# Attention to output projection: a fixed tail order, six prepared operand blocks, the last group's pieces spread by tick

## The chip, the cores and the metric

The kernel runs on one core of one Trainium2 chip. A core has TensorE (PE, the matrix multiplier), VectorE (DVE), ScalarE (ACT), GpSimd (POOL) and SyncE (SP), which here only issues DMAs. The metric is device time in microseconds of one execution. The kernel before has a median of 2857.04 us over 3 runs (2854.59 to 2858.03).

## The reference

Two post-norm layers with different token mixers, on x of 1024 positions by 1024 channels, all in fp32. What the change touches is the first layer's mixer and the projection behind it:

```python
proj = (x @ w_in).reshape(B, S, N_GROUPS, 3, ATTN_HEADS, ATTN_HEAD_DIM)
for g, (window, dilation) in enumerate(((128, 1), (512, 4), (2048, 16))):
    q = rotary(proj[:, :, g, 0], pos)
    k = rotary(proj[:, :, g, 1], pos)
    o, lse = dilated_window_attention(q, k, proj[:, :, g, 2], window, dilation)
wts = softmax(lse over the three g)               # per position and head
o = sum over g of wts[g] * o[g]
y = o.reshape(B, S, 1024) @ w_out
x = layer_norm(ALPHA * x + y)
# then: squared-ReLU MLP, norm; HGRN2 mixer, norm; MLP, norm
```

Each query of dilation d sees itself and 128 keys (or what there are) at distances d, 2d and so on. There are 16 heads of 64 channels.

## The kernel before, in words

Heads are taken in pairs (128 channels, one tile). A **unit** is one pair at one dilation; 24 units are worked in 12 groups of two. The input projection of a group is 21 **products** (252 in all, numbered n); each is 12 matmuls of 128x512 (L666 to L668: high by high, low by high and high by low part of fp32 operands that `split` makes, ACT for the high half at L137, DVE for the low at L138). Seven combined products stand for eight quarter blocks, and DVE and ACT put them together into e (q and k before rotary, L701) and vT.

While a group's products run, the attention of the group before is worked between them. The functions of that work are:

- `rope`: four DMAs on SP copy e with its halves exchanged into rot; DVE multiplies by cos into qT or kT (L472), multiplies rot by sin (L473) and adds (L474). With dilation 4 the DVE writes are strided.
- `pieces`: qk (L500, PE) gives s; a DVE instruction, called stt here, adds the mask and takes the maximum (L511); ACT takes exp (L514); ptr (L524) transposes p on PE; pv (L539) multiplies by v; ACT copies out to og (L547, L550); vtrans transposes v. Six pieces are one unit's `core`.
- `combine_tr`: transposes the statistics (mpt on PE) and sends them through DRAM (mdram) into ml.
- `combine` and `combine_mul` are the mix of a pair's three dilations: maxima, exp, sum, reciprocal and products on rows of 16 (L592 to L605), split into fh and fl (L611), six DMAs on SP spread them out into frow (L616), PE broadcasts a row to the heads' channels (fb, L626), DVE multiplies og by it and adds (L627 to L630).

Each of these steps is put at a product by tables of offsets from the group's base: `ROPES`, `OFFS`, `STATS` and `MIX`, and `ROPES0` for the rope steps of the last group's units, as far as they come before its end. In that loop `in_order` ties PE and DVE to the order in which the code issues; SP, ACT and POOL are ordered by a scheduler.

The **tail** is the attention of the last group's two units (a, dilation 4, and b, dilation 1), the last mixes and the output projection. Mixed output goes to DRAM by pair, in blocks oN[k]; `Out.load` reads a block back (onr) and `split_k` splits it (aoh, aol); the weight blocks wor are loaded and split by `load_w` and `split_w` (woh, wol), in halves of 512 columns (dm 0 and 1). One output tile (t, dm) of 128x512 is the sum over k of three matmuls (`rows`, L183 to L185). `stage_a` makes partial sums with the blocks that are there: tiles (0,0), (1,0), (2,0) side by side over six blocks, then (0,1), (1,1), (2,1), (3,0), (3,1) one by one, and adds ALPHA times the residual into z (L933). After each block's three matmuls `tick` runs some of the waiting steps, from lists that are spread evenly:

```python
ticks = 3 * nka + 5 * 7
def tick():
    count[0] += 1
    while fill and count[1] * ticks < count[0] * total:
        for f in fill.pop(0):
            f()
        count[1] += 1
```

`order.__exit__()` comes before the tail, so there the scheduler chooses the order of all engines. `fin(t)` makes a tile's remaining blocks and its layer norm, `tr(t)` the transposes for the MLP. Three blocks' first half (PREA = 3) are loaded and split in the last products; the others as the tail begins. U takes one of NSLOT = 50 buffers of 4 KB a partition; wp holds p-like work tiles in 3 buffers.

Of the kernel before, what the change touches and what calls it, by code (L numbers as in the profile page):

```python
# [10 lines left out]
F32R = mybir.dt.float32r  # L11
# [5 lines left out]
P = 128  # L17
# [12 lines left out]
RMS_EPS = 1e-6  # L30
CH = 64
NCH = S // CH
NSLOT = 50
NPRE = 2
PREA = 3
SPILL = (6, 5)
NKA = (6, 7)
EARLY = (2, 0)
# [16 lines left out]
       (30, 31, 33, 34, 35, 37, 38, 39, 41, 41, 42, 42, 42, 43))  # L55
STATS = ((12, 13, 15), (21, 22, 24))
ROPES = ((-5, -3, -3, -1, 1, 2), (5, 7, 7, 9, 11, 11))
ROPES0 = ((-5, -2, -1, 2), (-4, 0, 1, 4))
OFFS = ((1, 3, 5, 7, 9, 11), (10, 12, 14, 16, 18, 20))


# [1 line left out]
def trunk_kernel(  # L63
# [24 lines left out]
    nc = tc.nc  # L88
    cp = ctx.enter_context(tc.tile_pool(name="cp", bufs=1))
    up = ctx.enter_context(tc.tile_pool(name="up", bufs=NSLOT))  # L90
    wp = ctx.enter_context(tc.tile_pool(name="wp", bufs=3))
    sp = ctx.enter_context(tc.tile_pool(name="sp", bufs=4))
    ps = ctx.enter_context(tc.tile_pool(name="ps", bufs=1, space=bass.MemoryType.PSUM))
    dp = ctx.enter_context(tc.tile_pool(name="dp", bufs=1, space=bass.MemoryType.DRAM))
# [4 lines left out]
    def bank(tag, name):  # L99
        return ps.tile([P, 512], F32, name=name, tag=tag, bufs={"mm": 3, "s": 2, "pt": 2, "o": 1}[tag])  # L100
# [221 lines left out]
    def attention(pre, hc):  # L322
# [150 lines left out]
            return qT, (lambda: nc.vector.tensor_mul(rot, rot, sinT),  # L473
                        lambda: nc.vector.tensor_add(cls(qT, g), cls(qT, g), nat(rot, g)))  # L474

        def pieces(pr, g, qT, kT, vT, og, sS):
            st = {}

            def has_prev(b):
# [49 lines left out]

            def pv(b):  # L530
                if b % 4 == 0:
                    st["o"] = bank("o", "o")
                o = st["o"]
                pts = st.pop(("pt", b))
                nb = 2 if has_prev(b) else 1
                for i in range(nb):
                    kb = b - nb + 1 + i
                    for h in range(2):
                        nc.tensor.matmul(o[h * HD:(h + 1) * HD, (b % 4) * P:(b % 4 + 1) * P],  # L539
                                         st["vn"][:, kb * P + h * HD:kb * P + (h + 1) * HD],  # L540
                                         pts[:, (h * nb + i) * P:(h * nb + i + 1) * P],
                                         start=i == 0, stop=i == nb - 1, skip_group_check=True)
                if b % 4 == 3:
                    hb = b // 4
                    d = DIL[g]
                    if d == 1:
                        act(og[:, hb * 512:(hb + 1) * 512], o, AF.Copy)  # L547
                    else:
                        r = d // 2
                        act(og.rearrange("p (n r) -> p r n", r=d)[:, hb * r:(hb + 1) * r, :],  # L550
                            o.rearrange("p (r n) -> p r n", r=r), AF.Copy)

            return [
                [lambda: qk(0), vtrans],
                [lambda: qk(2), lambda: ptr(0), lambda: ptr(1)],
# [150 lines left out]
        def unit_work(gi, a, base):  # L706

            pr, g = groups[gi][a]
            if pr not in ml:
                ml[pr] = small([16, 2, NG, P], "ml", 1)  # L710
                ogs[pr] = [None] * NG
            sS = small([P, 2, 2, 8], "stats", 3)

            adds = {}

            def rope_of(t):
                res[a, t], adds[t] = rope(ep.pop((gi, a, 0 if t == 1 else 1)), g, "qT" if t == 0 else "kT")

            def begin():
                ogs[pr][g] = U("og")  # L720
                p = pieces(pr, g, res.pop((a, 0)), res.pop((a, 1)), ep.pop((gi, 2, a)), ogs[pr][g], sS)
# [18 lines left out]
        order.__enter__()  # L740
        load_x("21", 0, (L, R))
        first_w(0, R)
        load_x("21", 1, (L, R))
# [16 lines left out]
                low_w(n)  # L760
        for n in range(len(seq)):
            gi, i, j = seq[n]
            load_w(n + LOADW)
            if j == 0 and n // 3 < 6:
                get_T(n // 3 + 1, 1)
# [7 lines left out]
                constants2()  # L773
            if n == 36:
                hc.append(hgrn_consts())
            if n == len(seq) - 2 * PREA - 3:
                early = pre(oN)
            if n >= len(seq) - 2 * PREA - 1:
                next(early, None)
            if n == 0:  # L780
                get_T(2, 0)
# [7 lines left out]
            if n % 21 == 14:  # L789
# [3 lines left out]
                for a in range(2):  # L793
# [14 lines left out]
                    for k, f in zip(MIX[a], mix):  # L808
                        at(base + k, f)
                if last:  # L810
                    for a in range(2):
                        for k, f in list(zip(ROPES0[a], tail[a][0])):
                            if k < -1:
                                at(base + k, f)
                                tail[a][0].remove(f)
        order.__exit__()
        (ra, ca, sa, _), (rb, cb, sb_, mx) = tail
        done = [f for n in sorted(fill) for f in fill[n]]
        mine = [[ra[0]], [rb[0], rb[1]], [ra[1]], [ca[0], rb[2]], [ca[1]], [cb[0]], [ca[2]], [cb[1]], [ca[3]], [cb[2]],
                [ca[4]] + sa, [cb[3]], [ca[5]], [cb[4]] + sb_, [cb[5]], mx[:1], mx[1:3], mx[3:5], [],  # L820
                mx[5:7], mx[7:10], mx[10:]]
        lists = [done[k:k + 1] + (mine[k] if k < len(mine) else []) for k in range(max(len(done), len(mine)))]
        return oN, lists


    class Out:
# [9 lines left out]
            self.split_w(k, 0)  # L836

        def pre_steps(self, oN):
            for k in range(PREA):
                self.load(k, oN, 0)  # L840
                raw = U("wor")
                self.w[k] = (None, None, raw)
                nc.sync.dma_start(raw[:, :512], self.w_dram[k][:, :512])

            def steps():
                for k in range(PREA):
                    raw = self.w[k][2]
                    hi, lo = U("woh", F32R), U("wol", F32R)
                    self.w[k] = hi, lo, raw
                    split(raw[:, :512], hi[:, :512], lo[:, :512])  # L850
                    yield
                    self.split_k(k, 0)
                    yield

            return steps()

        def split_w(self, k, dm):
            hi, lo, raw = self.w[k]
# [24 lines left out]
                self.split_k(k, 0)  # L883


    def outproj_ln(pr, oN, fill, resid, gB_ap, bB_ap, keep):
        a = {}
        w = pr.w
        xo = pr.xo
# [6 lines left out]
        for k in range((PREA, NPRE)[pr.mixer], nka):  # L896
            pr.load(k, oN, 0)
            pr.load_w(k)
            split_k(k, 0)
        for k in range(nka):  # L900
            pr.split_w(k, 1)
        z = []

        def load_z(t):
# [11 lines left out]
        ticks = 3 * nka + 5 * 7  # L916

        def tick():
            count[0] += 1
            while fill and count[1] * ticks < count[0] * total:  # L920
                for f in fill.pop(0):
                    f()
                count[1] += 1
# [14 lines left out]
        def second(n):  # L938
            for _ in range(n):
                if ahead and len(oN) > ahead[0]:  # L940
                    k = ahead.pop(0)
                    pr.load(k, oN, 1)
                    split_k(k, 1)

        ks = list(range(nka))
        stage_a([(0, 0), (1, 0), (2, 0)], ks)
        for n, (t, dm) in enumerate([(0, 1), (1, 1), (2, 1), (3, 0), (3, 1)]):
            load_z(max(t, 1) + 1)
            if n in (1, 3) and len(w) < NK:
                k = len(w)  # L950
                pr.load_w(k)
                pr.split_w(k, 1)
            k = len(ks)
            if k < 7 and len(oN) > k and k < len(w):
                pr.raw[k] = oN[k]
                split_k(k, 0)
                ks = ks + [k]
            stage_a([(t, dm)], ks)
            if n >= EARLY[pr.mixer]:
                second(2)  # L960
# [4 lines left out]
        while fill:  # L965
            for f in fill.pop(0):
                f()
        for k in range(len(ks), NK):
# [4 lines left out]
        second(NK)  # L973
        xn = Fast(name + "f")

        def tr(t):
# [15 lines left out]
                nc.sync.dma_start(keep[t * P:(t + 1) * P, :], z[t])  # L992

        fin(0)
        fin(4, (0,))
        fin(1)
        fin(4, (1,))
        fin(2)
        fin(5, (0,))
        fin(3)  # L1000
        tr(0)
        fin(5, (1,))
        tr(1)
        tr(2)
        fin(6, (0,))
# [476 lines left out]
    def hgrn(xs, late, consts, pre, gw):  # L1482
# [101 lines left out]
        for hd in range(8):  # L1584
# [61 lines left out]
            for i in range(3):  # L1646
# [13 lines left out]
    x5d = dp.tile([S, D], F32, name="x5d")  # L1660
    pr = Out(w_attn_out, "a", 0)
    hc = []
    oN, fill = attention(pr.pre_steps, hc)
    xf, late = outproj_ln(pr, oN, fill, lambda t: x[t * P:(t + 1) * P, :],
                          ln_mix_g[0], ln_mix_b[0], x1d)
# [5 lines left out]
    xf, late = outproj_ln(pr, oN, fill, lambda t: x3d[t * P:(t + 1) * P, :],  # L1671
                          ln_mix_g[1], ln_mix_b[1], x5d)
    ffn(1, xf, late, x5d, ln_ffn_g[1], ln_ffn_b[1], True)

# [76 lines left out]
```

## Time and profile before

| what | value |
|---|---|
| median of 3 runs | 2857.04 us (2854.59 to 2858.03) |
| the profiled execution | 2856.82 us; its span 2854.6 us |
| mean granted TensorE clock | 0.995 |
| PE busy | 2789.4 us, 98% of the span |
| DVE, ACT, POOL busy | 2053.8, 1448.4, 122.6 us |
| share of PE in the chain that ended last | 90% |
| last product's last matmul (L668) | starts at 973.19 us |
| first matmul of the output projection (L183) | 973.42 us |

Times in rows of the trace are microseconds from the start of the span. A row of a timeline has the start, the duration, the engine, the line, the operation, and out<-in with the tile's names; in square brackets stand the idle time of the engine before it and what ended that. A row of the list of waits has the total, the number and the longest. A matmul's record lasts 0.39 us though one starts every 0.23 us, since they are pipelined; so what TensorE loses is read from the starts. `L` numbers are those of the kernel before; in the changed kernel the same lines lie 5 to 40 further down.

### The profile page before, as it was taken

Reading aid. Unit: us, or ns where it says so; the run is one execution under the profiler, and the core shown is the slowest. Engines: PE = TensorE matmul, PEld = TensorE weight load, DVE = VectorE, ACT = ScalarE, POOL = GpSimd, SP = SyncE. Lnnn points to the kernel's source line nnn. Section 1 sums busy time; section 2 is a strip of 40 time slices with the busy share of each in tenths; the row PEclk is TensorE's granted clock in tenths of the full one; section 3 lists DMA queues with packets and bytes.
Section 4 is the critical chain, followed back from the end, with each engine's and each line's share of the span. In section 5 each row is a group of like instructions: output and inputs, shape, how many; then the busy total and the mean of one; then the engine's idle time right before and its main releaser. Section 6 shows DMA issues by size and latency. Waiting matters only on the chain.

```text
span 2854.6 us, 39893 instructions
## 1 busy us (share of the span) xinstructions
PE 2789.4 (98%) x14152; PEld 2235.3 (78%) x14152; DVE 2053.8 (72%) x3830; ACT 1448.4 (51%) x3105; POOL 122.6 (4%) x67
## 2 busy tenths in 40 slices
PE   8999999999999989999999999999999999999998
PEld 6777777777777767888878887778787788878887
DVE  7768777776887767786686875555667787678677
ACT  5555555655555555544454444554553645454433
POOL 0000000000000003000000011111102200000000
PEclk9999999999999999999999999999999999999999
DMA  7766665666667523464584843101131455475654
GB/s 291 249 201 193 190 197 171 215 206 204 198 198 222 154 77 133 156 220 156 173 303 126 275 142 104 38 30 60 51 120 71 159 202 174 155 268 189 223 176 132
DMA packets 204935, 485.25 MB, mean 170 GB/s; under 512 B 29376, under 2 KB 43712, under 8 KB 204736
## 3 DMA queue, kind: packets, MB, share of 16 engines
q1 hardware_dynamic: 204736, 482.72, 51.3%
q8 instruction: 111, 1.82, 0.3%
q14 instruction: 88, 0.72, 0.1%
HBM read 362.82 MB, written 94.24 MB: 160 GB/s over the span
## 4 chain that ended last, share of the span: by engine, by line
PE 90%; DVE 4%; ACT 2%; DMA 1%; issue 1%; POOL 0%; SPq 0%; DVEq 0%; POOLq 0%; ACTq 0%
PE pmm L666 8%; PE pmm L668 8%; PE pmm L667 8%; PE pup L1114 7%; PE pup L1112 7%; PE pup L1113 7%; PE pdy L1264 4%; PE pdy L1260 4%; PE pdy L1263 4%; PE pmm L171 3%; PE s L500 3%; PE pdx L1263 3%; PE pdx L1264 3%; PE pdx L1260 3%; PE pmm L173 3%; PE pmm L172 3%
## 5 line engine op out<-in xcount | busy, mean ns | idle before, releaser
L666 PE MATMUL pmm<-xh,H 128*128 128x512 f32 x1008 | 407.7, 404 | 12.0 <-ACT H L432 8.5
L668 PE MATMUL pmm<-xh,H 128*128 128x512 f32 x1008 | 396.4, 393 | 0.0
L667 PE MATMUL pmm<-xl,H 128*128 128x512 f32 x1008 | 396.1, 393 | 0.0
L666 PEld LDWEIGHTS pmm<-xh,H 128*128 128x128 f32 x1008 | 191.2, 190 | 52.3 <-ACT H L432 8.5
L668 PEld LDWEIGHTS pmm<-xh,H 128*128 128x128 f32 x1008 | 190.4, 189 | 41.9 <-DVE H L440 0.3
L667 PEld LDWEIGHTS pmm<-xl,H 128*128 128x128 f32 x1008 | 191.1, 190 | 36.9
L514 ACT ACTIVATE p<-p,stats 128x128 f32<-128x128 f32 (+1 forms) x384 | 168.3, 441 | 92.6 <-DVE stats L511 92.2
L1263 PE MATMUL pdy<-dT,dS 128*128 128x512 f32 x512 | 199.2, 389 | 0.0
L1260 PE MATMUL pdy<-dT,dS 128*128 128x512 f32 x512 | 199.2, 389 | 0.0
L1264 PE MATMUL pdy<-dT,dS 128*128 128x512 f32 x512 | 199.2, 389 | 0.0
L511 DVE CUSTOM_DVE_ANT_0 p<-s,mask 128x128 f32<-128x128 f32 (+1 forms) x384 | 113.2, 347 | 68.4 <-PE s L500 58.8
L137 ACT ACTIVATE dS<-dr 128x512 fp32r<-128x512 f32 x192 | 119.5, 622 | 73.3 <-PE pdy L1264 36.6
L171 PE MATMUL pmm<-f0nh,wh 128*128 128x512 f32 x384 | 153.1, 399 | 0.0
L173 PE MATMUL pmm<-f0nh,wl 128*128 128x512 f32 x384 | 149.8, 390 | 0.0
L172 PE MATMUL pmm<-f0nl,wh 128*128 128x512 f32 x384 | 149.6, 390 | 0.0
L138 DVE TENSOR_TENSOR dS<-dr,dS 128x512 fp32r<-128x512 f32 x192 | 135.1, 703 | 16.5 <-ACT dS L137 16.5
L214 POOL TENSOR_TENSOR z<-z,bB 128x1024 f32<-128x1024 f32 x24 | 58.5, 2442 | 1687.8 <-ACT z L213 1678.3
L527 ACT ACTIVATE pts<-ppt 128x256 f32<-128x256 f32 (+1 forms) x192 | 85.3, 474 | 62.7 <-PE ppt L524 60.5
L137 ACT ACTIVATE dT<-hold 128x512 fp32r<-128x512 f32 x128 | 80.0, 625 | 69.5 <-DVE hold L1239 28.8
L1073 ACT ACTIVATE H<-wc 128x512 fp32r<-128x512 f32 x128 | 77.2, 625 | 74.6 <-DVE wc L1066 43.9
L1263 PEld LDWEIGHTS pdy<-dT,dS 128*128 128x128 f32 x512 | 96.1, 188 | 20.0
L1264 PEld LDWEIGHTS pdy<-dT,dS 128*128 128x128 f32 x512 | 96.1, 188 | 20.0
(395 smaller groups left out, 6927.9 us busy)
## 6 DMA issues: line engine op xcount, KB each, us to landing
xh<-xtd SPq DMA_DIRECT2D x110, 512.0 KB
xl<-xtd SPq DMA_DIRECT2D x110, 512.0 KB
dr<-hd SPq DMA_DIRECT2D x192, 256.0 KB
dr<-in_w_down_dram SPq DMA_DIRECT2D x128, 256.0 KB
rot<-e SPq DMA_DIRECT2D x192, 128.0 KB
wa<-in_w_up_dram SPq DMA_DIRECT2D x48, 512.0 KB
wb<-in_w_attn_dram SPq DMA_DIRECT2D x36, 512.0 KB
wa<-in_w_attn_dram SPq DMA_DIRECT2D x33, 512.0 KB
```

The lines of the kernel that those rows point to most:

```text
L171: nc.tensor.matmul(o, wh[:, k], xs.h(k), start=k == 0, stop=False)
L172: nc.tensor.matmul(o, wh[:, k], xs.l(k), start=False, stop=False)
L173: nc.tensor.matmul(o, wl[:, k], xs.h(k), start=False, stop=k == NK - 1)
L666: nc.tensor.matmul(o, wh, hi[k // 2][:, c], start=begin and k == 0, stop=False, skip_group_check=True)
L667: nc.tensor.matmul(o, wh, lo[k // 2][:, c], start=False, stop=False, skip_group_check=True)
L668: nc.tensor.matmul(o, wl, hi[k // 2][:, c], start=False, stop=end and k == 3, skip_group_check=True)
L1112: nc.tensor.matmul(o, wh, xf.h(b, k), start=begin and k == 0, stop=False, skip_group_check=True)
L1113: nc.tensor.matmul(o, wh, xf.l(b, k), start=False, stop=False, skip_group_check=True)
L1114: nc.tensor.matmul(o, wl, xf.h(b, k), start=False, stop=end and k == 3, skip_group_check=True)
L1260: nc.tensor.matmul(o[q], h, T_[:, L], start=begin, stop=False, skip_group_check=True)
L1263: nc.tensor.matmul(o[q], h, T_[:, R], start=False, stop=False, skip_group_check=True)
L1264: nc.tensor.matmul(o[q], l, T_[:, L], start=False, stop=end, skip_group_check=True)
```

## The change

1. **Order.** PE and DVE stay tied to the issue order to the end of stage A, and SP too from product 228 (PINSP).
2. **Six blocks.** `pre_steps` loads and splits the first half of six onr blocks and all of six wor blocks (one DMA of 128x1024 where there were two of 128x512), one split per product from n = 234 on. One slot less (NSLOT 49), one wp buffer more.
3. **Stage A by single tiles.** (0,0), (1,0), (2,0), (0,1), (1,1), (2,1) with six blocks, then (3,0), (3,1), (4,0), (4,1) with seven: 64 ticks. Each tick has its events: rope, core, statistics, mix, loads, splits.
4. **The last units.** Three of their rope steps come sooner (ROPES0); what is left, the end of kT, is at ticks 1 (a) and 5 (b). Cores are at ticks 3 to 33 and 6 to 36, the last mix at 38 to 55; the pieces take ptr ahead of qk, and the second unit's pv uses a bank of "mm". The mix of the last group but one moves (MIX0), some of it into the first ticks.
5. **The end.** fin and tr in another order; tile 4 is then partly done.

The numbers of PE, DVE and ACT instructions are the same in both kernels.

```diff
-NSLOT = 50
+NSLOT = 49
-PREA = 3
+PREA = 6
+PINSP = 228
-ROPES0 = ((-5, -2, -1, 2), (-4, 0, 1, 4))
+MIX0 = (20, 21, 21, 22, 23, 25, 26, 27, 27, 28, 29, 30, 30, 31)
+ROPES0 = ((-5, -2, -2, 0), (-4, -1, -1, 0))
+TCORE = ((3, 9, 15, 21, 27, 33), (6, 12, 18, 24, 30, 36))
+TROPE = (1, 5)
+TSTATS = ((25, 26, 30), (28, 29, 33))
+TMIX = (38, 40, 41, 43, 44, 48, 49, 50, 51, 52, 53, 54, 55, 55)
...
-    wp = ctx.enter_context(tc.tile_pool(name="wp", bufs=3))
+    wp = ctx.enter_context(tc.tile_pool(name="wp", bufs=4))
...
-                    st["o"] = bank("o", "o")
+                    st["o"] = bank("mm" if last == 2 else "o", "o")
...
+            if last:
+                return [
+                    [lambda: qk(0), vtrans],
+                    [lambda: ptr(0), lambda: ptr(1), lambda: qk(2)],
+                    [lambda: pv(0), lambda: pv(1), lambda: ptr(2), lambda: ptr(3), lambda: qk(4)],
...
+            if n == PINSP:
+                queue.__enter__()
...
-            if n == len(seq) - 2 * PREA - 3:
+            if n == len(seq) - 3 * PREA - 4:
                 early = pre(oN)
-            if n >= len(seq) - 2 * PREA - 1:
+            if n >= len(seq) - 3 * PREA - 4:
                 next(early, None)
...
-        order.__exit__()
...
+        for n in sorted(fill):
+            on([3 * (n - len(seq))] * len(fill[n]), fill[n])
+        on(TROPE, (ra[0], rb[0]))
+        for a, (core, stats) in enumerate(((ca, sa), (cb, sb_))):
+            on(TCORE[a], core)
+            on(TSTATS[a], stats)
+        on(TMIX, mx)
+        return oN, events, (order, queue)
...
         def tick():
+            if orders:
+                for f in fill.pop(count[0], []):
+                    f()
+                count[0] += 1
+                return
...
+            for n, k in enumerate((6, 7)):
+                on(4 + 6 * n, lambda k=k: pr.load_raw(k))
+                for dm in range(2):
+                    on(26 + 12 * n + 2 * dm, lambda k=k, dm=dm: pr.split_raw(k, dm))
+            for k in range(6):
+                on(4 * k, lambda k=k: pr.load(k, oN, 1))
+                on(19 + 3 * k, lambda k=k: split_k(k, 1))
+            for n, k in enumerate((6, 7)):
+                on(32 + 24 * n, lambda k=k: (pr.load(k, oN, 0), split_k(k, 0)))
+                on(34 + 23 * n, lambda k=k: split_k(k, 1))
+            for t, dm in [(0, 0), (1, 0), (2, 0), (0, 1), (1, 1), (2, 1), (3, 0), (3, 1), (4, 0), (4, 1)]:
+                load_z(max(t, 1) + 1)
+                stage_a([(t, dm)], list(range(6 if t < 3 else 7)))
...
         fin(0)
+            fin(1)
+            fin(5, (0,))
+            fin(2)
+            fin(5, (1,))
+            fin(3)
+            tr(0)
+            fin(4)
```

More of the change, by code (lines that the diff above doesn't have):

```diff
@@ L474, in rope, with pieces @@
                         lambda: nc.vector.tensor_add(cls(qT, g), cls(qT, g), nat(rot, g)))
-        def pieces(pr, g, qT, kT, vT, og, sS):
+        def pieces(pr, g, qT, kT, vT, og, sS, last):
             st = {}
@@ L720, in begin @@
                 ogs[pr][g] = U("og")
-                p = pieces(pr, g, res.pop((a, 0)), res.pop((a, 1)), ep.pop((gi, 2, a)), ogs[pr][g], sS)
+                p = pieces(pr, g, res.pop((a, 0)), res.pop((a, 1)), ep.pop((gi, 2, a)), ogs[pr][g], sS,
+                           a + 1 if gi == len(groups) - 1 else 0)
                 for f in p[0]:
@@ L740, in attention @@
         order.__enter__()
+        queue = in_order((mybir.EngineType.SP,))
         load_x("21", 0, (L, R))
@@ L807, in attention @@
                         at(base + k, f)
-                    for k, f in zip(MIX[a], mix):
+                    for k, f in zip(MIX0 if gi == len(groups) - 2 else MIX[a], mix):
                         at(base + k, f)
@@ L812, in attention, with on @@
                         for k, f in list(zip(ROPES0[a], tail[a][0])):
-                            if k < -1:
+                            if k < 0:
                                 at(base + k, f)
                                 tail[a][0].remove(f)
-        order.__exit__()
         (ra, ca, sa, _), (rb, cb, sb_, mx) = tail
[L818 to L823, printed above, removed]
+        events = {}
+        def on(ts, fs):
+            for t, f in zip(ts, fs):
+                events.setdefault(t, []).append(f)
+        for n in sorted(fill):
[6 more added lines that the diff above has]
+        return oN, events, (order, queue)
     class Out:
@@ L838, in pre_steps, with load_raw, split_raw @@
         def pre_steps(self, oN):
[L839 to L855, printed above, removed]
+            for n in range(3 * PREA + 4):
+                k, step = divmod(n, 3)
+                if step == 0 and k < PREA:
+                    self.load(k, oN, 0)
+                    self.load_raw(k)
+                if n >= 4:
+                    k, step = divmod(n - 4, 3)
+                    if step == 1:
+                        self.split_k(k, 0)
+                    else:
+                        self.split_raw(k, step // 2)
+                yield
+        def load_raw(self, k):
+            self.w[k] = (U("wor"),)
+            nc.sync.dma_start(self.w[k][0], self.w_dram[k])
+        def split_raw(self, k, dm):
+            if dm == 0:
+                self.w[k] = (U("woh", F32R), U("wol", F32R)) + self.w[k]
+            hi, lo, raw = self.w[k]
+            c = slice(dm * 512, dm * 512 + 512)
+            split(raw[:, c], hi[:, c], lo[:, c])
+            if dm == 1:
+                self.w[k] = (hi, lo)
         def split_w(self, k, dm):
@@ L883, in pre, with outproj_ln @@
                 self.split_k(k, 0)
-    def outproj_ln(pr, oN, fill, resid, gB_ap, bB_ap, keep):
+    def outproj_ln(pr, oN, fill, orders, resid, gB_ap, bB_ap, keep):
         a = {}
@@ L895, in outproj_ln @@
         nka = NKA[pr.mixer]
[L896 to L901, printed above, removed]
+        if not orders:
+            for k in range(NPRE, nka):
+                pr.load(k, oN, 0)
+                pr.load_w(k)
+                split_k(k, 0)
+            for k in range(nka):
+                pr.split_w(k, 1)
         z = []
@@ L943, in second, with tail, on @@
                     split_k(k, 1)
+        def tail():
+            def on(t, f):
+                fill.setdefault(t, []).append(f)
+            for n, k in enumerate((6, 7)):
[11 more added lines that the diff above has]
+                stage_a([(t, dm)], list(range(6 if t < 3 else 7)))
+            assert not fill, sorted(fill)
+            for o in orders:
+                o.__exit__()
+        if orders:
+            tail()
         ks = list(range(nka))
-        stage_a([(0, 0), (1, 0), (2, 0)], ks)
-        for n, (t, dm) in enumerate([(0, 1), (1, 1), (2, 1), (3, 0), (3, 1)]):
+        if not orders:
+            stage_a([(0, 0), (1, 0), (2, 0)], ks)
+        for n, (t, dm) in enumerate([] if orders else [(0, 1), (1, 1), (2, 1), (3, 0), (3, 1)]):
             load_z(max(t, 1) + 1)
@@ L967, in outproj_ln @@
                 f()
-        for k in range(len(ks), NK):
+        for k in range(len(ks), NK if not orders else 0):
             pr.raw[k] = oN[k]
@@ L972, in outproj_ln @@
         bB = bcast_rows(bB_ap, "bB")
-        second(NK)
+        if not orders:
+            second(NK)
         xn = Fast(name + "f")
@@ L994, in outproj_ln @@
         fin(0)
[L995 to L1002, printed above, removed]
+        if orders:
+            fin(1)
[5 more added lines that the diff above has]
+            fin(4)
+        else:
+            fin(4, (0,))
+            fin(1)
+            fin(4, (1,))
+            fin(2)
+            fin(5, (0,))
+            fin(3)
+            tr(0)
+            fin(5, (1,))
         tr(1)
@@ L1662, in trunk_kernel @@
     hc = []
-    oN, fill = attention(pr.pre_steps, hc)
-    xf, late = outproj_ln(pr, oN, fill, lambda t: x[t * P:(t + 1) * P, :],
+    oN, fill, orders = attention(pr.pre_steps, hc)
+    xf, late = outproj_ln(pr, oN, fill, orders, lambda t: x[t * P:(t + 1) * P, :],
                           ln_mix_g[0], ln_mix_b[0], x1d)
@@ L1670, in trunk_kernel @@
     oN, fill = hgrn(xs, late, hc, pr.pre, gw)
-    xf, late = outproj_ln(pr, oN, fill, lambda t: x3d[t * P:(t + 1) * P, :],
+    xf, late = outproj_ln(pr, oN, fill, None, lambda t: x3d[t * P:(t + 1) * P, :],
                           ln_mix_g[1], ln_mix_b[1], x5d)
```

4 lines of the change are left out of this document (added).

## The prediction

> **What bounds the kernel now.** The page is read first, for the busy shares of the engines.
>
> ```profile
> span 2854.6 us, 39893 instructions
> PE 2789.4 (98%) x14152; PEld 2235.3 (78%) x14152; DVE 2053.8 (72%) x3830; ACT 1448.4 (51%) x3105; POOL 122.6 (4%) x67
> ```
>
> TensorE is busy for 98% of the span, so a change that leaves its matmuls alone can win only where it waits or runs at a lower granted clock. The table of 10-us stretches is read next, over the tail of attention. Its columns are length, busy time (and count) of each engine, granted TensorE clock, DMA share and GB/s.
>
> ```profile
> core 0: us, PE busy (x) PEld busy (x) DVE busy (x) ACT busy (x) POOL busy (x), PEclk, DMA share, GB/s
> 1040.00:1050.00 10.00, 6.42 (x29) 4.58 (x29) 9.44 (x19) 4.60 (x9) 0.00 (x0) 0.92 0.48 161
> 1050.00:1060.00 10.00, 8.13 (x28) 5.79 (x28) 5.87 (x12) 1.57 (x3) 0.00 (x0) 0.84 0.30 81
> 1060.00:1070.00 10.00, 9.38 (x22) 5.74 (x22) 9.07 (x17) 1.28 (x3) 0.00 (x0) 0.56 0.23 84
> ```
>
> The third row is the surprising one: PE is 94% busy, with half the matmuls of a full stretch, because the clock stands at 0.56. Then the waits of TensorE between 972 and 1072 us (total, times, longest), and its timeline for the places.
>
> ```profile
> PE pmm L183 <- ACT aoh L137: 4.0, 2, 3.6
> PE fb L626 <- DMA frow<-fh: 1.9, 1, 1.9
> PE pmm L183 <- DVE z L933: 1.3, 1, 1.3
> PE pmm L183 <- DVE vT L701: 0.8, 1, 0.8
> PE o L539 <- ACT og L550: 0.7, 2, 0.4
> PE s L500 <- DVE kT L474: 0.5, 1, 0.5
> ```
>
> ```profile
> 973.19 0.39 PE L668 MATMUL pmm<-xh,H 128*128 128x512 f32 x1
> 973.42 0.39 PE L183 MATMUL pmm<-woh,aoh 128*128 128x512 f32 x1
> ...
> 1047.61 0.50 PE L183 MATMUL pmm<-woh,aoh 128*128 128x512 f32 x1 [3.58 <-ACT aoh L137]
> ...
> 1048.34 0.80 PE L185 MATMUL pmm<-woh,aol 128*128 128x512 f32 x1
> ...
> 1051.49 0.51 PE L183 MATMUL pmm<-woh,aoh 128*128 128x512 f32 x1
> ...
> 1057.75 0.70 PE L626 MATMUL fb<-frow,bsel 128*128 128x512 f32 x2 [1.87 <-DMA frow<-fh]
> ...
> 1058.52 0.59 PE L184 MATMUL pmm<-wol,aoh 128*128 128x512 f32 x1
> ...
> 1068.51 0.53 PE L185 MATMUL pmm<-woh,aol 128*128 128x512 f32 x1
> ```
>
> The last product of attention starts its last matmul at 973.19; the output projection's first follows at 973.42 (one every 0.23 us at full clock). I call 973.4 T0.
>
> **What the change removes.** The six lines add up to 9.2 us; a wait also leaves some 0.1 us before the next matmul's start, and there are eight, so I take 10. Two stretches run at half clock. From 1048.34 to 1051.49 eight matmuls take 3.15 us instead of 1.8: 1.4 us. From 1058.52 to 1068.51, 19 matmuls (4 of them fb) and one wait of 0.5 us take 10 us instead of 4.3 (19 x 0.227); less that wait, which is in the 10 already, 5.2 us. The new order removes the causes of all six: the operand blocks that aoh L137 split late are split in the last group, z is loaded sooner, and each core piece has a tick of its own. **Removed: 10 + 1.4 + 5.2 = 16.6 us.** That is the most that the tail can give; numbers of instructions on PE, DVE and ACT stay as they are.
>
> **What it adds, wait A.** From here the rows are of VectorE, whose order in the tail is now fixed to the order in which the code issues. They start just ahead of T0.
>
> ```profile
> 970.89 0.28 DVE L511 CUSTOM_DVE_ANT_0 p<-s,mask 128x128 f32<-128x128 f32 x1
> 971.11 2.35 DVE L473 TENSOR_TENSOR rot<-rot,sinT 128x1024 f32<-128x1024 f32 x2
> 973.38 2.05 DVE L474 TENSOR_TENSOR qT<-qT,rot 128x1024 f32<-128x1024 f32 x1
> 975.33 1.03 DVE L701 TENSOR_TENSOR vT<-pmm,vp 128x512 f32<-128x512 f32 x1
> 976.20 0.35 DVE L592 TENSOR_TENSOR mn<-ml 16x128 f32<-16x128 f32 x1
> ...
> 977.08 0.40 DVE L593 TENSOR_TENSOR mn<-mn,ml 16x128 f32<-16x128 f32 x1
> 978.01 0.88 DVE L595 TENSOR_TENSOR ml<-mn,ml 16x128 f32<-16x128 f32 x3
> 978.80 0.67 DVE L138 TENSOR_TENSOR wol<-wor,woh 128x512 fp32r<-128x512 f32 x1
> 979.40 1.21 DVE L474 TENSOR_TENSOR qT<-qT,rot 128x1024 f32<-128x1024 f32 x1
> 980.54 0.54 DVE L598 TENSOR_TENSOR ml<-ml 16x384 f32<-16x384 f32 x1
> 982.81 0.37 DVE L600 TENSOR_TENSOR mn<-ml 16x128 f32<-16x128 f32 x1
> 983.22 0.39 DVE L601 TENSOR_TENSOR mn<-mn,ml 16x128 f32<-16x128 f32 x1
> 983.65 0.94 DVE L603 RECIPROCAL mn<-mn 16x128 f32<-16x128 f32 x1
> 984.62 0.88 DVE L605 TENSOR_TENSOR ml<-ml,mn 16x128 f32<-16x128 f32 x3
> 991.25 2.02 DVE L472 TENSOR_TENSOR kT<-e,cosT 128x1024 f32<-128x1024 f32 x1
> ```
>
> In the kernel before, 18 ticks of matmuls lie between T0 and qk(0) of unit a, so its kT wait is the 0.5 us of the list. In the changed one qk(0) stands at tick 3. Up to it TensorE has 12 projection matmuls (2.7 us), four pv, four ppt and a statistics transpose with the friction between them (1.5 us): it asks for kT at T0 + 4.2 = 977.6.
>
> VectorE's queue in the changed order, from the stt that ends at 971.1 (that one waits for TensorE's s, so it isn't sooner or later than here): one rot product 1.2, the strided qT add 1.95 (973.38 to 975.33), the kT product that was at 991.25 before, 1.9, one wol split 0.6. So vT starts at 976.8, against 975.33. Then vT 0.9; the mix of the last but one group, L592, L593, L595 (x3) 1.6; rot, qT add and kT product of unit b, 1.2 + 1.15 + 1.15; L598, L600, L601, L603, L605 (x3) 0.5 + 0.4 + 0.4 + 0.95 + 0.8; and only then rot 1.2 and the strided kT add 1.95 of unit a. That is 12.2 us, to 989.0. TensorE stands from 977.6 to 989.0, **A = 11.4 us.** Behind it wait vtrans, all later ticks and, through them, ACT and the statistics: nothing else can fill it, for the order of PE is fixed too. Low end 8 us, if VectorE were at vT at T0; high end 13, with a microsecond or two of backlog from the twelve more splits (0.6 each) that now lie in the last group. That backlog I take as nothing: VectorE waited 9.6 us for s between 895 and 955, in the row below, and of its total work little is added ahead of T0, as the later ones drop out of it.
>
> ```profile
> L511 DVE CUSTOM_DVE_ANT_0 p<-s,mask 128x256 f32<-128x256 f32 (+1 forms) x20 | 6.5, 379 | 9.6 <-PE s L500 9.6
> ```
>
> **Half clock behind A.** Both long waits above (3.6 and 1.9 us) were followed within about a microsecond by a stretch at half clock. One of 3.2 to 3.4 us costs 1.4 to 1.7. I take **1.6**; the ends are 0.9 and, by the long stretch, 5.1.
>
> The Trainium skill (TensorE: Matmul & The Clock Gate, Part 1: The HAM clock gate) has one idle window of about 3.4 us close the gate and one busy window open it, in a free-running window. The trace agrees on the length of a stretch (1048.34 to 1051.49) but shows 1.87 us to be enough for a drop at 1058.5. By the page's rule as it stands A drops the clock once and B, below, perhaps not at all; the sum would be 1.6 us lower.
>
> **Small ones.** qk(0) of unit b at tick 6 comes out even: kT of b is ready about 4 us after A ends, TensorE is there in 4.2. A ppt behind the first fb must wait for the og product, since there are two such banks: 0.9 us (fb, then one product of 0.7 and its start). The second unit's pv has a bank of its own now, so the L550 wait doesn't come back. One slot less and a fourth wp buffer: nothing, as each wor block is split soon after it lands.
>
> **Wait B, at tick 48.** The last mix starts on VectorE behind the z addition of tick 35; call its end on PE X. z 0.6, L592 to L595 1.6, two splits 1.2, L598 to L605 3.05, one z 0.6, fl 0.55: 7.6 us. Then the issues on SP and the landing.
>
> ```profile
> 1055.63 0.61 SPq L616 DMA_DIRECT2D frow<-fl  x1
> ```
>
> Six issues stand 0.65 us apart, of which the first is out ahead of fl: X + 10.6 for the start of the last. From 1055.63 to the fb at 1057.75 it took 2.1 us: X + 12.7. TensorE has 12 ticks of 0.68 us and 1.6 us of pv until it needs fb: X + 9.8. **B = 2.9 us**, between 2 and 4 (a split or a z addition more or less on the chain, and the issue's spread), and half clock behind it, at the short stretch's price, **1.6** (0 to 5.1; the fb's lie a tick apart now, so the short one is nearer).
>
> **Sum.** Added: 11.4 + 1.6 + 0.9 + 2.9 + 1.6 = 18.4 us. Removed: 16.6. The end of the tail (fin, the transposes) has the same work in another order and I cost that at nothing: VectorE is the same number of instructions behind the last z. Net +1.8 on the profiled execution's 2856.8 us (span 2854.6 and 2.2 around it), which is 0.2 below the median of 2857.0: **2858.6 us.** With the bounds (added 8 + 0.9 + 0.9 + 2 to 13 + 5.1 + 0.9 + 4 + 5.1) the sum goes from -4.8 to +11.5.
>
> **The rivals.** The measurement can tell 0.2%, that is 5.7 us, from no change.
>
> *Forecast, no change within 0.2%:* A takes what the six waits gave. For it: A's terms are rows, and the order is fixed. 0.42.
>
> *Slower: the clock stays low.* Where it decides: the first 10 us behind A. There TensorE has qk, eight transposes and short ppt's with DVE and ACT between them, and at 1058.5 such a mixture, after only 1.87 us of idling, kept half clock for 10 us instead of 3.2. If any wait of 0.5 us lies there (kT of b is even to within that), the long price comes twice: 2 x 3.5 us more, 2858.6 + 7 = 2866. Against it: more 128x512 matmuls lie between than at 1058. 0.35, with late loads on the SP queue, whose order is now fixed from the 229th product on, in the same case.
>
> *Faster: A at its floor and no B.* A is 8 us if VectorE comes to vT at T0; B goes if fl comes 3 us sooner, as it would if the z additions and the two splits in its way (2.4 us) were done while VectorE waits, and its half clock goes with it. 8 + 1.6 + 0.9 - 16.6 = -6.1: 2850.7. Against it: VectorE had no idle time from 970.9 to 985, so A's queue can't well be shorter. 0.23.
>
> *It doesn't do what it says:* the six blocks are split but wor lands late, and aoh or woh L137 is waited for again. 512 KB per block is asked for 7 products ahead; it is within the slower case.
>
> **How the numbers follow.** The range takes the forecast's bounds and the larger part of both rivals: 2847 to 2868. Chances: faster 0.23, same 0.42, slower 0.35.
>
> **What would show it.** Right: one wait of s on DVE kT of about 11 us that starts near 977, with the granted clock at half behind it; no wait on aoh L143 near 1043; one of fb on frow of 2 to 4 us near tick 48; 44 matmuls in 10 us elsewhere. Wrong: a kT wait under 8 us (the VectorE queue was misread, then the change is faster by the difference), or stretches at 0.5 clock that last over 5 us (slower), or waits of the products ahead of T0, which the kernel before doesn't have.

## The result and the profile after

The changed kernel takes **2863.24 us** (median of 12 runs, 2858.84 to 2867.85), the kernel before 2857.31 in the runs beside it: ratio 1.0021, 95% interval 1.0012 to 1.0030. That is 5.9 us or 0.21% slower, just past the 0.2% that I took as the bound of no change. The forecast was 2858.6, so 4.6 us are to be explained. The profiled execution is the slowest of the twelve: 2867.85 us, 11.0 more than before's.

The first page lines of the changed kernel:

```profile
span 2866.1 us, 39906 instructions
PE 2787.6 (97%) x14152; PEld 2237.8 (78%) x14152; DVE 2052.1 (72%) x3832; ACT 1448.7 (51%) x3105; POOL 121.7 (4%) x67
```

TensorE has as many instructions as before and is busy for 1.8 us less, so all of the difference is waiting or clock. (VectorE has two instructions more, 3832 for 3830: additions into z, of which the new stage A makes 18 where there were 16.) Its 10-us stretches (columns as in the prediction):

```profile
940.00:950.00 10.00, 7.30 (x41) 5.83 (x39) 6.12 (x15) 6.26 (x16) 0.00 (x0) 0.79 0.68 249
950.00:960.00 10.00, 10.00 (x61) 7.76 (x60) 6.59 (x16) 6.81 (x20) 0.00 (x0) 0.87 0.48 148
...
980.00:990.00 10.00, 5.51 (x31) 3.74 (x29) 9.86 (x13) 1.95 (x8) 0.00 (x0) 1.00 0.93 296
990.00:1000.00 10.00, 2.89 (x14) 2.24 (x15) 8.54 (x20) 1.33 (x6) 0.00 (x0) 0.51 0.11 42
...
1060.00:1070.00 10.00, 7.60 (x28) 6.20 (x29) 5.60 (x9) 0.63 (x1) 0.00 (x0) 0.83 0.45 162
...
1110.00:1120.00 10.00, 8.10 (x41) 6.39 (x40) 4.63 (x11) 5.42 (x13) 2.40 (x1) 0.99 0.62 217
```

Two of these four holes were forecast: 980 to 1000 with half clock in it (wait A) and 1060 to 1070 (wait B). Two were not: 940 to 960, ahead of the tail, and 1110 to 1120, in the end of it. TensorE's waits between 972 and 1080 us confirm the first two:

```profile
PE s L506 <- DVE kT L480: 11.4, 1, 11.4
PE fb L641 <- DMA frow<-fh: 2.8, 1, 2.8
PE ppt L530 <- ACT pts L533: 0.9, 1, 0.9
PE ppt L530 <- DVE og L642: 0.7, 1, 0.7
```

Where the time went is read from the starts of the same matmul in both traces. First the kernel before: product 228, the 193rd matmul of the projection, the first of the MLP. Up to the 193rd, TensorE has the same matmuls of each kind in both kernels.

```profile
879.95 0.48 PE L666 MATMUL pmm<-xh,H 128*128 128x512 f32 x1
...
1070.03 0.39 PE L183 MATMUL pmm<-woh,aoh 128*128 128x512 f32 x1
...
1118.34 0.39 PE L1112 MATMUL pup<-af11h,H 128*128 128x512 f32 x1
```

Then the same three and others of the changed one:

```profile
880.43 0.48 PE L681 MATMUL pmm<-xh,H 128*128 128x512 f32 x1
...
946.36 1.97 PE L545 MATMUL o<-pts,vn 128*64 128x128 f32 x16 [2.70 <-ACT og L553]
...
980.88 0.39 PE L683 MATMUL pmm<-xh,H 128*128 128x512 f32 x1
...
997.11 1.66 PE L506 MATMUL s<-kT,qT 64*128 64x128 f32 x8 [11.35 <-DVE kT L480]
...
1075.38 0.39 PE L189 MATMUL pmm<-woh,aoh 128*128 128x512 f32 x1
...
1119.32 0.50 PE L189 MATMUL pmm<-woh,aoh 128*128 128x512 f32 x1 [1.90 <-DVE z L1054]
...
1126.49 0.39 PE L1186 MATMUL pup<-af11h,H 128*128 128x512 f32 x1
```

| stretch | before | changed | difference | forecast |
|---|---|---|---|---|
| product 228 to the last product's last matmul | 93.2 | 100.5 | **+7.2** | 0 |
| from there to the 193rd matmul of the projection | 96.8 | 94.5 | **-2.3** | +1.8 |
| from there to the MLP's first matmul | 48.3 | 51.1 | **+2.8** | 0 |

Behind that the MLP's first 336 matmuls lose 1.2 us more and what follows, to the start of the last matmul, 2.5 (1643.6 to 1646.1). Several of these items change from run to run. In other kernels whose products are the same, the first stretch took 98.5 to 99.3 us, and the last part 1642 to 1645. In act_order, sp_free and mix_sooner, below, whose end is the same, the third stretch took 49.2 to 49.4 us, only 0.9 to 1.1 more than before, and the MLP lost nothing: their waits for z of 1.6 to 1.7 us left the clock at 1.00. With 98.5 for the first stretch and nothing for the last part the sum is 5.3 - 2.3 + 2.8 + 1.2 = 7.0 us, and with the cheaper end 5.3 - 2.3 + 1.0 = 4.0; the medians' 5.9 lies between.

### The profile page after: what moved, and what is told of

It reads as the page before. It is cut to its first block, busy times and chain, and to the rows that moved or that the text cites. A ratio compares the mean times of both kernels' runs of the same rounds, so it can differ in the third digit from the quotient of the medians.

```text
span 2866.1 us, 39906 instructions
## 1 busy us (share of the span) xinstructions
PE 2787.6 (97%) x14152; PEld 2237.8 (78%) x14152; DVE 2052.1 (72%) x3832; ACT 1448.7 (51%) x3105; POOL 121.7 (4%) x67
## 3 DMA queue, kind: packets, MB, share of 16 engines
q1 hardware_dynamic: 203584, 482.71, 51.1%
```

## The experiments

Two theories stood at the start. **Mine:** three separate places, products 237 to 243 (ACT and DVE, loaded with the early splits), the late z in fin, and waits A and B as forecast. **The rival:** one cause, SP's fixed order, which makes loads late everywhere. All ratios below are to the kernel before in the same runs.

**The hole at 943 us.** ACT's and DVE's timelines of the changed kernel show what stood ahead of pv:

```profile
943.70 0.60 ACT L712 ACTIVATE e<-pmm 128x512 f32<-128x512 f32 x1 [2.12 <-PE pmm L683]
944.20 1.14 ACT L143 ACTIVATE aoh<-onr 128x512 fp32r<-128x512 f32 x2
945.24 0.59 ACT L710 ACTIVATE e<-pmm 128x512 f32<-128x512 f32 x1
945.71 0.60 ACT L553 ACTIVATE og<-o 128x512 f32<-128x512 f32 x1
```

```profile
944.85 0.69 DVE L144 TENSOR_TENSOR aol<-onr,aoh 128x512 fp32r<-128x512 f32 x1 [3.84 <-ACT aoh L143]
945.46 0.42 DVE L517 CUSTOM_DVE_ANT_0 p<-s,mask 128x256 f32<-128x256 f32 x1
```

pv needs the o bank, which the og copy empties; ACT had put that copy behind an e copy that waits 2.1 us for TensorE's own product, and behind two splits of the early blocks. DVE stood 3.84 us for the same aoh, with the stt behind it.

*act_order.* `in_order` for ACT as well, from product 228 to the last one:

```diff
+        loop = in_order((mybir.EngineType.Activation,))
...
+                loop.__enter__()
...
+        loop.__exit__()
         (ra, ca, sa, _), (rb, cb, sb_, mx) = tail
```

> ACT too is tied to the issue order from product 228 to the last product (not in the tail). Theory: the 2.7 us in which pv waited for og L553 at 943 us, with half clock behind it, came because ACT's order had the copy to og behind an e copy that waits for TensorE's next product, and two aoh splits of the early blocks behind the same copy. Then the last 15 products come back by 4 to 7 us: 2857 to 2860. Rival, the data of the early blocks come late because SP's order is fixed from product 228: aoh still waits, no gain, about 2863. A third possibility, ACT in issue order waits in other places: later than 2865.

Measured: 2862.65 us, ratio 1.0017 (1.0008 to 1.0026). The og wait went, and others came. Waits of TensorE from 900 to 1000 us:

```profile
PE s L506 <- DVE kT L480: 11.2, 1, 11.2
PE o L545 <- ACT pts L533: 3.1, 3, 1.6
PE mpt L579 <- ACT pts L533: 2.2, 2, 1.8
```

The stretch from product 228 still took 98.5 us. The order of ACT chooses which wait is seen; it isn't what makes the loss. The time is the rival's, but not by the rival's way, since the wait that it was to keep has gone.

*sp_free.* SP left to the scheduler (the three lines of `queue` out).

> SP is left to the scheduler; PE and DVE stay tied. Theory: SP's fixed order isn't what costs: same waits, 2861.5 to 2864.5. Rival: loads pass the waiting stores and rot copies, and the waits of products 237 to 243 or the kT wait go: under 2860.

Measured: 2862.59 us, 1.0016 (1.0007 to 1.0025), the same waits to 0.2 us. The rival theory falls: SP's fixed order costs nothing here that these runs can tell.

*late_splits.*

```diff
-            if n == len(seq) - 3 * PREA - 4:
+            if n == len(seq) - 11:
                 early = pre(oN)
-            if n >= len(seq) - 3 * PREA - 4:
+            if n >= len(seq) - 11:
+                next(early, None)
                 next(early, None)
```

> The early blocks' 18 splits are made at two per product from n = 243 to 251 instead of one per product from 234 on; loads start at n = 241. Theory: the 18 extra splits on ACT and DVE, not one queue's order, hold ptr, s, H and og of products 237 to 243 up, 5.3 us with half clock behind the longest (tying ACT's order only moved that to other waits). Without them there, these products come back to the pace of the kernel before: 3 to 5 us, 2858.5 to 2860.5. Rival: VectorE and ACT are as full in 243 to 251, the loss moves there or into the wait for kT at tick 3: 2862 to 2865.

Measured: 2863.28 us, 1.0022 (1.0012 to 1.0032). Product 228 and the last product of late_splits, then its waits:

```profile
881.90 0.48 PE L681 MATMUL pmm<-xh,H 128*128 128x512 f32 x1
...
975.69 0.39 PE L683 MATMUL pmm<-xh,H 128*128 128x512 f32 x1
```

```profile
PE s L506 <- DVE kT L480: 14.6, 1, 14.6
```

93.8 us, all but 0.6 of the loss is gone: the splits in products 237 to 243 are its cause. And the rival that I gave with it is right as well: the kT wait is 3.2 us longer, the stretch from the last product to the 193rd matmul 6.3 longer (100.8), the wait for z in fin 3.3 us instead of 1.9, and the time is the same. VectorE has to make these splits before kT in either case; they are paid where they are put.

**Wait A.** *mix_sooner:* MIX0 begins (17, 18, 18, 19, 20, 25, ...).

> The first five mix steps of the last group but one (L607 to L631) come three products sooner (MIX0 17, 18, 18, 19, 20). Theory: the 11.4 us wait for kT at tick 3 is the sum of VectorE's queue, 5.6 us of which are these steps; VectorE was busy for only 4.3 us between 960 and 970. The wait falls to 6 to 9 us and the time by 2.5 to 5.5 us: 2858 to 2861. Rival, VectorE comes to the last vT later by as much: wait and time unchanged, 2863.

Measured: 2864.96 us, 1.0030 (1.0018 to 1.0042). From 900 to 1000 us:

```profile
PE s L506 <- DVE kT L480: 8.0, 1, 8.0
PE o L545 <- ACT og L553: 2.7, 1, 2.7
PE o L545 <- ACT pts L533: 1.1, 1, 1.1
PE ppt L530 <- ACT p L520: 1.0, 2, 0.9
```

The kT wait fell as the sum says, within the 6 to 9 us given, but pv and ppt ahead of it waited about 2 us that they had not, vtrans behind it 0.7, and the time did not fall.

*cores_later:* TCORE, TSTATS, TMIX and block 7 by 12 ticks, tiles (5, 0) and (5, 1) in stage A, z of tile 7 sooner.

> Both last units' cores, statistics, mix and block 7 come 12 ticks later, and stage A makes tile 5's partial sums as well (78 ticks); residual 7 is asked for after fin(1), as in z_sooner. To compare with z_sooner, 2859.4. Theory: qk(0) reaches TensorE 8.2 us later, VectorE's 12.2 us are done meanwhile: the kT wait falls from 11.3 to about 3 us, half clock behind it goes, and the later mix has room enough: 8 to 10 us less, 2849 to 2852. Rival: the whole chain of the last mix ends later, and fin of block 7 waits for it: 2858 to 2861.

Measured: 2869.47 us, 1.0046 (1.0033 to 1.0058). Its waits from 972 to 1080 us:

```profile
PE fb L641 <- DMA ml<-mdram: 9.6, 1, 9.6
PE fb L641 <- DMA frow<-fl: 5.3, 1, 5.3
```

VectorE's and SP's timelines ahead of the first of them, whose fb starts at 1003.38:

```profile
998.07 0.53 DVE L626 TENSOR_TENSOR fl<-ml,fh 16x384 fp32r<-16x384 f32 x1
```

```profile
1001.30 0.61 SPq L631 DMA_DIRECT2D frow<-fl  x1
```

No wait for kT at all, and 9.6 us at the next thing that VectorE makes: the first fb of the older mix, at tick 12. (The list names a load of ml, which SP issues only at 1002.39. What fb reads is frow, whose last copy goes out at 1001.30, behind an fl that VectorE makes straight after kT.) Both expectations missed, and the miss tells the most. While kT was the wait, that fb lay behind it and was never late.

*later_all* moves the older mix too (first step at tick 6, fb from tick 30), the last mix's fb five ticks more, block 6 to tick 50 and 7 to 76, with tiles 0 to 6 over six blocks each; *later_all_late* is the same with the splits of late_splits and cores 15 ticks later.

> As cores_later, 12 ticks later, but with what held that one up moved too: the whole mix of the last group but one (first step at tick 6 instead of 0, its fb from tick 30 instead of 12), the last mix's fb five ticks more, block 6 split at tick 50, block 7 at 76; stage A makes tiles 0 to 6 with six blocks each (84 ticks), z of 6 and 7 is asked for within it. The early splits stay at one per product. To compare with fb_and_z, 2855.5. Theory: the 11.3 us wait for kT is time in which VectorE's 12.2 us lie on the path; with 5.6 us of mix behind them and 8.2 us of matmuls beside them nothing is left of it, and the half clock behind it goes: 2842 to 2846. Rival: VectorE's total work is the bound of the stage, the wait comes back at qk(0) of b or at an fb: 2852 to 2857.

> The same with the early splits of late_splits (two per product from n = 243) and cores 15 ticks later. Theory: in late_splits the 5.3 us of products 237 to 243 came back and were lost again at the kT wait (14.6 for 11.4) and beside it; now that wait is covered but for about 3 us, so the products' 5 us stay won: 2839 to 2844. Rival: VectorE stays behind through the first 20 ticks, qk of a and b wait 5 us or more: 2846 to 2852.

Measured: 2857.76 us, 1.0000 (0.9991 to 1.0009), and 2860.31, 1.0009 (1.0000 to 1.0018). Of the waits of later_all from 972 to 1080 us the two long ones:

```profile
PE s L506 <- DVE stats L517: 4.2, 1, 4.2
PE vpt L494 <- ACT vn L495: 1.4, 1, 1.4
```

The kT wait's 11.4 us are down to 5.6, but the time is just above the rival's range (2852 to 2857) and far from the theory's 2842 to 2846. Against fb_and_z, below, nothing is left of the gain: the fuller end waits for POOL's norm, z and the MLP's weights instead (POOL z 1.6, z 1.3, DVE H 2.6 and ACT H 1.7 us). later_all_late missed both of its expectations: the products are back at 93.8 us, TensorE waits 3.1 us for s, 1.8 and 1.6 at ppt and z in stage A, and why it comes out 2.5 us behind later_all stays open.

**Wait B and the late z.** *fb_later:* the last mix's fb at ticks 53 to 60, block 7 at 61.

> The last mix's broadcasts (fb) and the split of block 7 come five ticks later (TMIX 53 to 60 for 48 to 55). Theory: fb waits 2.8 us for frow at tick 48 and half clock follows; five ticks are 3.4 us of matmuls, so both go: 2859 to 2860. Rival, the wait moves to the end of stage A or to fin, which needs block 7 (aoh L143): 2863 or later.

Measured: 2857.84 us, 1.0003 (0.9994 to 1.0012): 5.4 us less than the changed kernel, and no fb wait.

*z_sooner:*

```diff
             fin(1)
+            load_z(7)
             fin(5, (0,))
```

> The residuals of tiles 6 and 7 are asked for after fin(1) instead of in fin(6) and fin(7). Theory: they stood on SP behind the sixth store to x1d, which the new order of fin makes later; z L1054 held TensorE for 1.9 us at 1117 and half clock followed. Both go, 2 to 4 us: 2859 to 2861. Rival, the MLP's weights are still behind the stores and are the next wait: 2862 to 2863.

Measured: 2859.39 us, 1.0006 (0.9997 to 1.0015), 3.9 less, with no z wait. SP's timelines show where the loads stood, before and changed:

```profile
1076.88 25.07 SPq L992 DMA_DIRECT2D x1d<-z  x6
1102.04 1.21 SPq L907 DMA_DIRECT2D z<-in_x_dram  x2
```

```profile
1087.57 25.69 SPq L1057 DMA_DIRECT2D x1d<-z  x6
1113.32 1.25 SPq L942 DMA_DIRECT2D z<-in_x_dram  x2
```

In both the last two z loads stand behind six stores; TensorE is 5.4 us later at 1075, the loads are 11.3 us later, since the sixth store (1101.63 before, 1112.94 changed) waits for a norm that the new order of fin makes last. VectorE's row of the changed kernel shows who waited for them:

```profile
1118.58 1.29 DVE L1054 SCALAR_TENSOR_TENSOR z<-z,pmm 128x512 f32<-128x512 f32 x2 [2.82 <-DMA z<-in_x_dram]
```

*fb_and_z*, both edits:

> fb_later and z_sooner together. Theory, two separate places: -5.4 and -3.9 add up, about 2854 (2853 to 2856). Rival, the two share a cause (in fb_later the z wait was 1.5 us instead of 1.9): about 2857.

Measured: 2855.47 us, 0.9990 (0.9981 to 0.9999). The two add up to within 1.5 us (their sum would be 2853.9), so they are two places, as the theory had it.

**A version that is faster than both.** *gap_splits* is fb_and_z with

```diff
-                next(early, None)
+                for _ in range(1 if n < 240 else 0 if n < 244 else 1 + n % 2):
+                    next(early, None)
```

> fb_and_z (2855.5) with the early steps one per product to n = 239, none at 240 to 243, then one and two in turn from 244 to 251. Theory: the waits of products 237 to 243 come from the splits right there; VectorE and ACT have 2 to 4 us free in each of the products 244 to 249, so about 4 of the 5.3 us come back and the kT wait grows by 1 to 2 us: 2852 to 2854. Rival, as late_splits showed, VectorE gives all of it back at kT: 2855 to 2857.

Measured: **2853.53 us, 0.9984 (0.9976 to 0.9993)**, with 11 runs between 2852.93 and 2855.05. Two waits of gap_splits:

```profile
PE s L506 <- DVE kT L480: 11.6, 1, 11.6
PE o L545 <- ACT og L553: 1.7, 1, 1.7
```

The og wait is 1 us shorter and the kT wait has grown by only 0.3 us. The stretch from product 228 is 97.0 us. In fb_and_z it took 99.3, with half clock behind the og wait, and in fb_later, where the clock stayed at 1.00, 98.5: so 1.5 us are gained beside the clock. The medians of gap_splits and fb_and_z lie 1.9 us apart, but their runs overlap (fb_and_z: 2851.60 to 2858.72), so the size of this last step is less sure than that gap_splits beats both kernels.

*gap_and_3:* gap_splits with cores, statistics and the last mix three ticks later.

> gap_splits with cores and statistics three ticks later and the last mix as much (fb 56 to 62, block 7 at 63). Theory: the kT wait falls by the 2 us of matmuls, as far as VectorE is its only bound: 2 us under gap_splits. Rival: the end of the mix, now at the last ticks, holds fin (aoh L143) up by as much: no difference to gap_splits.

Measured: 2853.36 us, 0.9983 (0.9974 to 0.9992). The time is the rival's, no difference, but not by its way, since no wait for aoh in fin appears: kT waits 2.6 us less (9.0), and og (1.9 us more), fb (0.8) and z (0.4) take it back.

## Why the prediction missed its size

- **What bounds the kernel** was right: TensorE's busy time didn't move (2787.6 for 2789.4 us) and the whole difference lies in waits and clock.
- **Wait A** was right in place, cause and size: forecast 11.4 us, measured 11.4. VectorE's queue came out step by step:

```profile
979.15 1.22 DVE L479 TENSOR_TENSOR rot<-rot,sinT 128x1024 f32<-128x1024 f32 x1
...
984.76 1.06 DVE L716 TENSOR_TENSOR vT<-pmm,vp 128x512 f32<-128x512 f32 x1
...
993.92 1.20 DVE L479 TENSOR_TENSOR rot<-rot,sinT 128x1024 f32<-128x1024 f32 x1
995.15 1.91 DVE L480 TENSOR_TENSOR kT<-kT,rot 128x1024 f32<-128x1024 f32 x1
```

  From the rot product to vT 5.6 us (forecast 5.65), from vT to the end of kT 12.3 (12.2). TensorE asked for kT at 985.8, 4.7 us behind its T0 of 981.1 (forecast 4.2).
- **Wait B** was right: forecast 2.9, measured 2.8 us. The half clock behind A and B cost about 1.5 us each (forecast 1.6 each), read from the matmuls behind them. The rival of the long stretches came in length, but not in price: half clock began within A and lasted 10.2 us, 990.1 to 1000.3, and only the last 3.2 of them lay behind the wait.
- **Removed: 16.6 us** was too little. Added between the last product and the 193rd matmul were 11.5 + 1.5 + 0.7 + 2.9 + 1.4 = 18.0 us by the trace, and 0.9 that wasn't forecast (the ppt wait for pts); the stretch is 2.3 shorter, so about 21.2 went. The prediction's sum has no term for most of the rest. Outside of waits and half clock, TensorE loses time where one kind of matmul follows another: by my estimate from the starts (the time to the next start, less the usual distance of that kind) 9.0 us at 86 such changes in the kernel before, and 5.2 at 72 in the changed one. The new order saves 3.8 us there.
- **"That backlog I take as nothing"** is the step that failed. VectorE's idle time over 60 us was no cover, because in the products 237 to 243 themselves it and ACT had little left, and TensorE's order is fixed with one o bank: 7.2 us in the profiled execution, 5.3 to 6.1 in others. late_splits shows it (93.8 us without those splits there). The prediction had named waits of the products ahead of T0 among the signs that it is wrong.
- **"The end of the tail ... I cost that at nothing"** failed as well: the matmuls are the same, but two loads on SP stand behind a store that now waits longer. 2.8 us and the 1.2 behind in the profiled execution, 0.9 to 1.1 in others; z_sooner takes 3.9 off the median.
- **The faster rival** (A at its floor) didn't come; VectorE's queue was not shorter, as said against it.
- **That the sum came within 4.6 us** is in part luck: two terms put at nothing cost 6 to 11 us by the execution, and what was removed was put 4.6 us too low (21.2 for 16.6), which hid about half of that.

What stays open: how much of the 2.5 us behind the MLP's first 336 matmuls belongs to the change. Between kernels that part varied from -1.6 to +2.5 us. The profiled execution has 13.7 us of half clock there (1747.9 and 1812.7, 6.8 us each) where the kernel before has 6.8, and one wait (pdx for d3s) of 3.8 us instead of 2.3; the other kernels have 6.8 to 13.7 us of half clock there too.

## What to carry to other kernels

When a second engine's queue is full over a whole stage, moving its work sooner or later moves the wait; three experiments (mix_sooner, cores_later, gap_and_3) took 2.6 to 11.4 us off one wait and gave it back at other waits, above all at the next thing that the engine makes. What did gain was work that stood in a queue for no reason of its own: a broadcast asked for five ticks too soon, a load behind a store, and, by 1.5 us in the trace, splits that lay in the fullest products. Average idle time of an engine is no cover; look at the very products into which its new work falls, and at what stands behind the instruction that waits.

## What the runs showed of the hardware

The price of a wait depends on when it falls. In all 14 traces every stretch at half clock, but for the one that the end of the kernel cuts off, lasts 3.41 us or a whole multiple, and within a trace they all start on one grid of that step: in the changed kernel 945.73, 990.10, 1061.78 and 1119.81 lie 13, 21 and 17 steps apart. So the traces can be read window by window, with borders taken from their half-clock stretches, here around the wait for og, which was 2.70 us in both kernels. First the changed kernel, then fb_later (columns as in the prediction; the clock is the third from the end):

```profile
942.31:945.73 3.42, 1.35 (x6) 0.78 (x5) 0.88 (x2) 2.03 (x5) 0.00 (x0) 1.00 0.94 333
945.73:949.14 3.41, 2.78 (x20) 2.45 (x21) 3.41 (x11) 3.05 (x11) 0.00 (x0) 0.50 0.49 195
```

```profile
943.06:946.48 3.42, 1.90 (x9) 1.24 (x7) 0.34 (x1) 1.49 (x3) 0.00 (x0) 1.00 0.85 294
946.48:949.89 3.41, 2.18 (x24) 1.68 (x24) 3.41 (x12) 3.41 (x12) 0.00 (x0) 1.00 0.66 246
```

In the changed kernel 2.1 us of the wait fell into one window, and the next two were at half clock. In fb_later the border cut the wait into 1.5 and 1.2 us, and the clock stayed at 1.00. The stretch from product 228 took 98.5 us in the two kernels where it stayed (fb_later, z_sooner), 99.2 to 99.3 with one window at half clock (sp_free, fb_and_z, cores_later) and 100.5 with two. The 1.7 us of gap_splits was cut as well, so it doesn't show that such a wait is safe.

Over the windows at full clock of all 14 traces (11358, without each trace's beginning and end), half clock followed in each of the 70 that had more than 1.84 us without a matmul's record, in 8 of 21 with 1.46 to 1.84, and in none with less. At half clock, full clock came back only behind windows with at most 0.62 us idle. Idle time isn't all of it: the 10.2 us at half clock from 1058.6 in the kernel before are three windows with 0.1, 0.5 and 0.05 us idle, and the first of them did not end it.

The Trainium skill (TensorE: Matmul & The Clock Gate, HAM oscillation — how this bites in real kernels) gives the rule that TensorE must not stand for more than about 3.4 us. Here 1.9 us (z, at 1117) and 2.1 us in one window were enough, so by these traces a wait under 3.4 us isn't safe. The free-running window of about 3.4 us, which the prediction cited from the same page of the Trainium skill, agrees with the grid of 3.41 us and with the different price of the same wait. By the prediction's reading of that rule B would perhaps not drop the clock; its 2.8 us did, from 1061.8 to 1065.2.
